# Two of seven block products of a down projection, each split once more into seven half-size products

## The chip, the cores and the metric

The kernel runs on one core of a Trainium2 chip. The metric is the device time of one execution in microseconds; the median of 3 runs before the change was 1494.11 us (1493.38 to 1494.94). The engines are TensorE (PE: matmuls; PEld: loads of the stationary operand), VectorE (DVE), ScalarE (ACT), GpSimd (POOL), and SyncE (SP), whose queue issues the DMA transfers. SBUF is the on-chip memory, PSUM holds the matmul results.

## The reference

One layer of an encoder is applied to two batches, 512 and 1024 rows of 1024 numbers, with the same weights, in 32-bit floats. What matters here is the end of the layer:

```
h = rmsnorm(x, norm_ffn_g)
u = dwconv(h @ w_up, ffn_dw_w, ffn_dw_b)          # 1024 x 5632, convolution over 3 rows
x = x + (silu(u[..., :2816]) * u[..., 2816:]) @ w_down     # 2816 x 1024
return rmsnorm(x, norm_final_g)
```

`w_down` is the down projection: 1536 rows in all, a contraction over 2816 and 1024 columns out.

## The kernel before, in words

**Matmuls.** A product of 32-bit floats is taken as three matmuls in a reduced format. Every operand is split into a high part, which ACT casts, and a low part, which DVE or POOL subtracts; then high x high, high x low and low x high are added up in PSUM. One matmul has a stationary operand of 128 x 128 and a moving operand of up to 512 columns, and loads its own stationary operand.

**Stages.** Attention, convolution and output projection come first, with the prompt's up projection among them. From some 760 us on, the sample's up projection runs as a loop over 22 column tiles `j` (128 gate and 128 value columns; lines 1715 to 1749). It already uses Strassen's method in Winograd's form: `second`, `sixth`, `first`, `seventh`, `fifth`, `fourth`, `third` are seven block products in place of eight. The gated results are written to DRAM by `value_part` (line 1370) in the blocks and block sums that the down projection needs: `ga[i, p]` for product `i` and chunk `p`. For the prompt's rows the same lies in `gt` and `gb`.

**Down projection.** It is again seven block products, in the order 1, 2, 5, 6, 7, 4, 3 (`ORDER`, line 1520). So "the second product" is number 2 and "the sixth" is number 4. Each has 768 rows (512 of the sample's and 256 of the prompt's block), a contraction over 11 chunks of 128 (`NPAIR`), and 512 columns. Its weights are a quarter of `w_down`, or a sum of quarters that DVE makes in place (`operands`, line 1534).

`load_next` (line 1491) takes transfers from a list written out ahead (`ahead`) and issues them on SP's queue; `operands(i, p)` makes the splits for one chunk, in two to three pairs of an ACT cast and a DVE subtraction (lines 1096 and 1092, and 1563 for the prompt's rows); `make(k + lead)` keeps that 4 chunks ahead of TensorE (`LEAD`). `group(i, p, w)` (line 1664) is the six matmuls of one chunk for one of three row blocks `w` (256 rows each), in a two-bank PSUM tile `wide()`, of which there are four. After the last chunk `evacuate` (line 1595) adds the block to the running sums of Winograd's form, on DVE, ACT or POOL. `with_x` adds the residual rows that `load_x1` fetched, one third on DVE and two thirds on POOL. `product(i)` (line 1689) runs the groups, and issues these extra loads and additions at certain chunks of the products 7 and 4.

**Order and buffers.** From the last pass of the loop on, the order of the instructions on TensorE's and SP's queues is that of the program text; in the loop that holds for TensorE only; a planner orders the rest. Buffers come from one list of free slots (`Slots`, line 74: 61 of 2 KB and 15 of 4 KB a partition, and a few others). A tile takes the slot that has been free longest, and its first writer waits until the slot's last reader is done.

Of the kernel before, what the change touches and what calls it, by code (L numbers as in the profile page):

```python
# [9 lines left out]
F32 = mybir.dt.float32  # L10
# [163 lines left out]
def tile_hybrid_encoder(ctx: ExitStack, tc: tile.TileContext, xs, xsT, rel_bias, norm_attn_g, w_in,  # L174
# [1311 lines left out]

    pr, second_half = {}, {}
# [3 lines left out]
    def load_next(n):  # L1491
        for _ in range(n):
            if ahead:
                key, p = ahead.popleft()
                roomy = sum(f[0][0] in "qc" for f in sb.free) > 5
                if (key, p) in second_half:
                    t = second_half.pop((key, p))
                elif key in BRIEF and p % 2 == 0 and p + 1 < NPAIR and roomy:
                    both = sb.tile([2, NT])
                    t, second_half[key, p + 1] = Part(both, 0), Part(both, 1)  # L1500
                    both = None
                else:
                    t = sb.tile([NT])
                pr[key, p] = t
                what, i, n2 = key
                if what == "a":
                    src = ga[i, p][:]
                elif what == "g":
                    n = min(2, NPAIR - 2 * p)
                    for q in range(n):  # L1510
                        j, h = {1: (0, HL), 2: (1, HL), 4: (1, HR)}.get(i, (0, None))
                        src = gb[2 * p + q][:, GB[i], :] if h is None else gt[2 * p + q][:, j, h]
                        nc.sync.dma_start(t[:, q * HT:(q + 1) * HT], src)
# [7 lines left out]
    need = {1: B11, 2: B21, 5: B12, 6: B22, 4: B21, 3: B22}  # L1521
    for i in ORDER:
        for p in range(NPAIR):
            ahead.append((("a", i, 0), p))
            if i in need:
                ahead.append((need[i], p))
            if p % 2 == 0:
                ahead.append((("g", i, 0), p // 2))

# [4 lines left out]
    def operands(i, p):  # L1534
# [4 lines left out]
        a = pr.pop((("a", i, 0), p))  # L1539
        if i == 1:  # L1540
# [17 lines left out]
        hl[i, p] = (split_of(a[:], True), split_of(b[:], True))  # L1558
        if p % 2 == 0:
            g = pr.pop((("g", i, 0), p // 2))  # L1560
            n = slice(0, min(2, NPAIR - p) * HT)
            hi, lo = hp[i, p // 2] = sb.tile([NT], F32R), sb.tile([NT], F32R)
            nc.scalar.copy(hi[:, n], g[:, n])
            sub(lo[:, n], g[:, n], hi[:, n].bitcast(F32))

    steps = [(i, p) for i in ORDER for p in range(NPAIR)]
# [4 lines left out]
    def mm_down(out, i, p, tt):  # L1571
# [7 lines left out]
        nc.tensor.matmul(out, sh[:, c], th[:], start=(p == 0), stop=False)  # L1579
        nc.tensor.matmul(out, sh[:, c], tl[:], start=False, stop=False)  # L1580
        nc.tensor.matmul(out, sl[:, c], th[:], start=False, stop=(p == NPAIR - 1))  # L1581
# [73 lines left out]
    def make(k):  # L1655
        nonlocal made
        while made <= min(k, len(steps) - 1):
            i, p = steps[made]
            operands(i, p)
# [4 lines left out]
    def group(i, p, w, lead=LEAD):  # L1664

        k = ORDER.index(i) * NPAIR + p
# [5 lines left out]
        for q in range(2):  # L1672
            mm_down(pd[w][:, q * NT:(q + 1) * NT], i, p, 2 * w + q)
# [7 lines left out]

    filled = set()
# [5 lines left out]

    def product(i):
        rest = [(p, w) for p in range(2, NPAIR - 2) for w in range(NW3)]  # L1690
# [4 lines left out]
        for p, w in order:  # L1695
# [7 lines left out]
            if i == 4 and p == 2:  # L1703
                load_x1(1, 1)
                fins.append(sb.tile([D]))
                nc.sync.dma_start(fins[0][:], norm_final_g.partition_broadcast(P))
            if i == 4 and p == 4:
                with_x("e", 1, 1)
            if i == 4 and p == 6:
                load_x1(0, 1)  # L1710
            if i == 4 and p == 8:
                with_x("o12", 0, 1)
                load_x1(1, 0)

    for j in range(2, NJ):
# [43 lines left out]
    base = len(steps) - NPAIR  # L1759
# [86 lines left out]
```

## Time and profile before

| | |
|---|---|
| median of 3 runs | 1494.11 us |
| the profiled execution | 1490.76 us |
| its span, first to last instruction | 1489.0 us |
| mean granted TensorE clock | 0.999 |
| TensorE busy | 1471.2 us (99%) |
| DVE / ACT / POOL busy | 1138.2 / 797.0 / 676.7 us |
| matmuls | 6808 |
| moved by DMA | 225.08 MB, mean 151 GB/s |

A row of the profile names the line of the kernel, the engine, the operation, the tiles (out, then in, by their first letters) and the shape, then a count, the busy time and the mean of one in nanoseconds. "Idle before" is the time that the engine waited just before such an instruction, and the arrow names what ended the wait. In a timeline a row begins with its start and its length in microseconds, counted from the start of the span; "x4" are four instructions in one row. A view by stretch gives for each stretch its length and the busy time and the count of instructions of each engine.

### The profile page before, as it was taken

To read this page: it belongs to the slowest core of one execution; us is meant where nothing else is said; L and a number is where in the kernel's file an instruction comes from. 1 tells how busy PE (TensorE), PEld (TensorE's weight loads), DVE (VectorE), ACT (ScalarE), POOL (GpSimd) and SP (SyncE) were. 2 spreads that over 40 slices of the span, in tenths; PEclk is the share of its full clock that TensorE was granted. 3 is DMA by queue.
4 is the path that set the end of the run, shared out by engine and by line. 5 is a ranking of instruction groups with operands and counts; after the bars stand their busy time and mean duration, and the time that the engine had idled before them with its cause. 6 is when DMAs were issued, how large, how long until landed. Compare 5 with 4: busy or idle time off the path is not lost.

```text
span 1489.0 us, 19864 instructions
## 1 busy us (share of the span) xinstructions
PE 1471.2 (99%) x6808; PEld 1219.4 (82%) x6808; DVE 1138.2 (76%) x1616; ACT 797.0 (54%) x1417; POOL 676.7 (45%) x540
## 2 busy tenths in 40 slices
PE   9999999999999999999999999999999999999998
PEld 7788888888888888878888888888887888888886
DVE  5999996788689965766868777777776946569884
ACT  8555656346777776443465554455545633444254
POOL 6953335235665666754336555555544000003345
PEclk9999999999999999999999999999999999999999
DMA  9953246284333346784213333333332672357644
GB/s 315 294 168 86 86 121 194 89 244 130 122 107 121 127 140 209 248 283 168 71 57 107 106 107 106 107 106 102 102 102 84 224 265 85 112 172 232 214 165 170
DMA packets 221761, 225.08 MB, mean 151 GB/s; under 512 B 12331, under 2 KB 161843, under 8 KB 221532
## 3 DMA queue, kind: packets, MB, share of 16 engines
q1 hardware_dynamic: 221660, 223.82, 46.8%
q8 instruction: 53, 0.87, 0.3%
q14 instruction: 48, 0.39, 0.1%
HBM read 164.77 MB, written 60.05 MB: 151 GB/s over the span
## 4 chain that ended last, share of the span: by engine, by line
PE 88%; DVE 3%; DMA 3%; POOL 3%; ACT 2%; issue 1%; SPq 0%; POOLq 0%; ACTq 0%; DVEq 0%
PE w L1229 9%; PE w L1230 9%; PE w L1231 9%; PE w L1580 7%; PE w L1579 7%; PE w L1581 7%; PE u L347 5%; PE u L348 5%; PE u L350 5%; PE b L347 4%; PE b L350 4%; PE b L348 4%; PE u L842 2%; PE u L841 2%; PE u L840 2%; PE a L674 1%
## 5 line engine op out<-in xcount | busy, mean ns | idle before, releaser
L231 POOL TENSOR_TENSOR q<-q,q 128x1024 fp32r<-128x1024 f32 x71 | 172.0, 2428 | 118.9 <-ACT q L230 48.5
L1092 POOL TENSOR_TENSOR q<-q,q 128x512 fp32r<-128x512 f32 x101 | 142.7, 1420 | 148.4 <-ACT q L1215 137.6
L1092 DVE TENSOR_TENSOR h<-h,h 128x512 fp32r<-128x512 f32 (+2 forms) x202 | 157.0, 811 | 66.0 <-ACT h L1096 28.6
L1581 PE MATMUL w<-h,h 128*128 128x512 f32 x462 | 179.7, 389 | 0.0
L1579 PE MATMUL w<-h,h 128*128 128x512 f32 x458 | 178.2, 389 | 0.0
L1580 PE MATMUL w<-h,h 128*128 128x512 f32 x458 | 178.2, 389 | 0.0
L1229 PE MATMUL w<-h,q 128*128 128x512 f32 x448 | 174.9, 390 | 1.6 <-ACT w L1312 1.3
L1231 PE MATMUL w<-h,q 128*128 128x512 f32 x448 | 174.3, 389 | 0.0
L1230 PE MATMUL w<-h,q 128*128 128x512 f32 x426 | 165.8, 389 | 0.0
L402 DVE SCALAR_TENSOR_TENSOR c<-c,cvw,c 128x512 f32<-128x512 f32 x209 | 156.9, 751 | 3.1
L347 PE MATMUL u<-h,q 128*128 128x512 f32 x368 | 146.8, 399 | 1.9 <-DVE h L969 1.9
L348 PE MATMUL u<-h,q 128*128 128x512 f32 x368 | 144.0, 391 | 0.0
L350 PE MATMUL u<-h,q 128*128 128x512 f32 x360 | 141.2, 392 | 0.0
L1089 POOL TENSOR_TENSOR q<-q,q 128x1024 f32<-128x1024 f32 x12 | 32.8, 2742 | 230.0 <-DMA h<-gb 190.0
L1096 ACT CAST h<-h 128x512 fp32r<-128x512 f32 x120 | 71.9, 620 | 99.0 <-DVE h L1092 41.6
L347 PE MATMUL b<-h,q 128*128 128x512 f32 x264 | 104.9, 397 | 0.9 <-DVE q L437 0.9
L348 PE MATMUL b<-h,q 128*128 128x512 f32 x264 | 103.7, 393 | 0.0
L230 ACT CAST q<-q 128x1024 fp32r<-128x1024 f32 (+1 forms) x73 | 75.4, 1038 | 52.6 <-POOL q L231 22.1
L350 PE MATMUL b<-h,q 128*128 128x512 f32 x264 | 103.5, 393 | 0.0
L1581 PEld LDWEIGHTS w<-h,h 128*128 128x128 f32 x462 | 86.7, 188 | 18.0
L1579 PEld LDWEIGHTS w<-h,h 128*128 128x128 f32 x458 | 86.0, 188 | 18.0
L1580 PEld LDWEIGHTS w<-h,h 128*128 128x128 f32 x458 | 86.0, 188 | 17.7
(443 smaller groups left out, 3624.3 us busy)
## 6 DMA issues: line engine op xcount, KB each, us to landing
q<-in_w_up SPq DMA_DIRECT2D x88, 512.0 KB, 4.3
ga<-q SPq DMA_DIRECT2D x64, 256.0 KB, 2.0
h<-ga SPq DMA_DIRECT2D x57, 256.0 KB, 3.5
q<-in_w_in SPq DMA_DIRECT2D x28, 512.0 KB, 5.1
h<-in_w_down SPq DMA_DIRECT2D x52, 256.0 KB, 3.8
q<-in_x_sample SPq DMA_DIRECT2D x15, 512.0 KB, 6.4
h<-qsd SPq DMA_DIRECT2D x23, 256.0 KB, 3.5
x1d<-q SPq DMA_DIRECT2D x11, 512.0 KB, 4.8
```

What stands on the lines that cost most here:

```text
L231: ins = (nc.vector if dve else nc.gpsimd).tensor_tensor(lo[:], raw[:], hi[:].bitcast(F32), op=ALU.subtract)
L347: nc.tensor.matmul(out, whi[:, kc, :], hi[:], start=(kc == 0), stop=False)
L348: nc.tensor.matmul(out, whi[:, kc, :], lo[:], start=False, stop=False)
L350: nc.tensor.matmul(out, wlo[:, kc, :], hi[:], start=False, stop=(kc == KC - 1))
L402: nc.vector.scalar_tensor_tensor(acc[:], src(t), w(t), acc[:], op0=ALU.mult, op1=ALU.add)
L1092: (eng or nc.vector).tensor_tensor(out, a, b, op=ALU.subtract)
L1229: nc.tensor.matmul(out, whi[:, s], hi[:], start=(start and c == 0), stop=False, **go)
L1230: nc.tensor.matmul(out, whi[:, s], lo[:], start=False, stop=False, **go)
L1231: nc.tensor.matmul(out, wlo[:, s], hi[:], start=False, stop=(stop and c == 3), **go)
L1579: nc.tensor.matmul(out, sh[:, c], th[:], start=(p == 0), stop=False)
L1580: nc.tensor.matmul(out, sh[:, c], tl[:], start=False, stop=False)
L1581: nc.tensor.matmul(out, sl[:, c], th[:], start=False, stop=(p == NPAIR - 1))
```

## The change

Products 2 and 4 (`TWO`) are each taken by a second level of the same algorithm. The first ten chunks are paired, so the contraction is split into even and odd chunks, the 768 rows into two halves of 384 and the 512 columns into two of 256. That makes seven inner products in the order 1, 2, 6, 7, 4, 5, 3 (`INNER`), each with 5 chunk pairs (`NQ`), 3 blocks of 128 rows and 256 columns. The eleventh chunk goes through the old `group`.

The sums on the left side for the inner products 5, 6, 7 and 3 are made during the up projection (`two_step`, one call at the end of each pass of the loop, the rest behind it): `two_load` reads the blocks back from DRAM, `two_sums` makes four sums on POOL and stores them in `gl`. The sums of weights for inner product 6 and later are made in `inner` on POOL, four operations of 256 columns for each chunk pair. `inner` also splits the operands, 384 and 256 columns each. `product2` runs the matmuls, with copies and additions in PSUM between the inner products, and keeps the operands 7 sets ahead (`LEAD2`). The extra loads and additions of product 4 now follow its inner products number two to five in that order (`tails`).

```diff
+    TWO = (2, 4)
+    NQ = NPAIR // 2
+    HB = 3 * P
+    gl = {(i, k): dr.tile([P, NQ, HB], F32, name=f"gl{i}_{k}") for i in TWO for k in (5, 6, 7, 3)}
...
+    def two_load(i, q):
+        both = []
+        for p in (2 * q, 2 * q + 1):
+            t = sb.tile([2 * HB])
+            nc.sync.dma_start(t[:, 0:NT], ga[i, p][:])
+            nc.sync.dma_start(t[:, NT:2 * HB], prompt_part(i, p))
+            both.append(t)
+        return both
+
+    def two_sums(i, q, both):
+        (e0, e1), (o0, o1) = ([t[:].rearrange("p (w h c) -> p w h c", h=2, c=P)[:, :, h, :] for h in range(2)] for t in both)
+        gp = nc.gpsimd.tensor_tensor
+        gp(o1, e1, o1, op=ALU.add)
+        gp(e1, e0, e1, op=ALU.subtract)
+        gp(e0, o1, e0, op=ALU.subtract)
+        gp(o0, o0, e0, op=ALU.subtract)
+        for k, src in ((5, o1), (7, e1), (6, e0), (3, o0)):
+            nc.sync.dma_start(gl[i, k][:, q, :].rearrange("p (w c) -> p w c", c=P), src)
...
+    def two_step(j):
+        if two_got:
+            i, q, both = two_got.popleft()
+            two_sums(i, q, both)
+            both = None
+        if two_due and j > 4 * two_due[0][1] + 4:
+            i, q = two_due.popleft()
+            two_got.append((i, q, two_load(i, q)))
...
+                if what == "A":
+                    if (i, n2) in gl:
+                        nc.sync.dma_start(t[:], gl[i, n2][:, p, :])
+                        continue
+                    o, h = {1: (0, 0), 2: (1, 0), 4: (1, 1)}[n2]
+                    src = ga[i, 2 * p + o][:].rearrange("p (w h c) -> p w h c", h=2, c=P)[:, :, h, :]
+                    nc.sync.dma_start(t[:, 0:2 * P].rearrange("p (w c) -> p w c", c=P), src)
+                    nc.sync.dma_start(t[:, 2 * P:HB], prompt_part(i, 2 * p + o)[:, h * P:(h + 1) * P])
+                    continue
...
+    INNER = (1, 2, 6, 7, 4, 5, 3)
...
+    def inner(i, k, q):
+        while (("A", i, k), q) not in pr or (k in (1, 2) and i in need and (need[i], 2 * q + k - 1) not in pr):
+            load_next(1)
+        a = pr.pop((("A", i, k), q))
+        if k in (1, 2):
+            bt[k, q] = weights(i, 2 * q + k - 1)
+        e, o = bt[1, q], bt.get((2, q))
+        if k == 6:
+            t = t1[q] = sb.tile([HT])
+            gp = nc.gpsimd
+            sub(t[:], e[:, QR], e[:, QL], gp)
+            sub(e[:, QR], o[:, QR], e[:, QR], gp)
+            sub(e[:, QL], o[:, QR], t[:], gp)
+            sub(o[:, QL], o[:, QL], e[:, QL], gp)
+            t = None
...
+        ah, al, bb = sb.tile([HB], F32R), sb.tile([HB], F32R), sb.tile([2, HT], F32R)
+        nc.scalar.copy(ah[:], a[:])
+        sub(al[:], a[:], ah[:].bitcast(F32))
+        nc.scalar.copy(bb[:, 0, :], b)
+        sub(bb[:, 1, :], b, bb[:, 0, :].bitcast(F32))
+        h2l[k, q] = ah, al, bb
...
+    tails = {4: {1: last_weights, 2: lambda _=None: with_x("e", 1, 1), 3: lambda _=None: load_x1(0, 1), 4: last_x}}
...
+    LEAD2 = 7
+
+    def product2(i, between):
+        z = {}
+        C11, C12, C21, C22 = (slice(n * HT, (n + 1) * HT) for n in range(4))
+        kept = [sb.tile([2, HT]) for _ in range(NW3)]
+        for n, k in enumerate(INNER):
+            for w in range(NW3):
+                if n == 0:
+                    z[w] = wide()
+                s = {1: C11, 2: C11, 6: C22, 7: C22, 4: C21, 5: C12, 3: C12}[k]
+                out = z[w][:, s]
+                for q in range(NQ):
+                    if len(pr) < CAP and sum(f[0][0] == "h" for f in sb.free) > ROOM:
+                        load_next(1)
+                    make(place[i, k, 0] + (w * NQ + q) // 3 + LEAD2)
+                    ah, al, bb = h2l[k, q]
+                    c = slice(w * P, (w + 1) * P)
+                    go = dict(skip_group_check=True)
+                    nc.tensor.matmul(out, ah[:, c], bb[:, 0, :], start=(k == 1 and q == 0), stop=False, **go)
+                    nc.tensor.matmul(out, ah[:, c], bb[:, 1, :], start=False, stop=False, **go)
+                    nc.tensor.matmul(out, al[:, c], bb[:, 0, :], start=False, stop=(q == NQ - 1), **go)
...
+                if k == 1:
+                    nc.scalar.copy(z[w][:, C22], out)
+                elif k == 6:
+                    nc.scalar.copy(kept[w][:, 0, :], out)
+                elif k == 7:
+                    nc.scalar.copy(z[w][:, C21], out)
+                elif k == 5:
+                    nc.scalar.copy(kept[w][:, 1, :], out)
+                    add(z[w][:, C22], z[w][:, C22], kept[w][:, 1, :])
+                elif k == 3:
+                    add(out, out, kept[w][:, 0, :])
+                out = None
+            if n in between:
+                between[n]()
...
+        for w in range(NW3):
+            group(i, NPAIR - 1, w)
...
     def product(i):
+        if i in TWO:
+            product2(i, tails.get(i, {}))
+            return
...
         third(j)
         split_up(j + 1, 3)
+        two_step(j)
     fill((3, 0), (3, 1), (4, 0), (4, 1))
     sb.free.extend(raws.free)
     value_part(NJ - 1)
+    while two_due or two_got:
+        two_step(NJ)
```

More of the change, by code (lines that the diff above doesn't have):

```diff
@@ L1528, in tile_hybrid_encoder @@
                 ahead.append((("g", i, 0), p // 2))
+    place = {step: n for n, step in enumerate(steps)}
     hl, hp = {}, {}
@@ L1569, in tile_hybrid_encoder, with mm_down @@
     NW3 = 3
-    def mm_down(out, i, p, tt):
+    def mm_down(out, i, p, tt, more=False):
         (sh, sl), (th, tl) = hl[i, p]
@@ L1657, in make @@
         while made <= min(k, len(steps) - 1):
-            i, p = steps[made]
-            operands(i, p)
+            (inner if len(steps[made]) == 3 else operands)(*steps[made])
             made += 1
```

87 lines of the change are left out of this document (58 added, 29 removed).

## Prediction

> **What bounds the kernel now.** I read the page's busy lines and its chain first, then busy time by stretch for the two block products that change, then single instructions there.
>
> ```profile
> span 1489.0 us, 19864 instructions
> PE 1471.2 (99%) x6808; PEld 1219.4 (82%) x6808; DVE 1138.2 (76%) x1616; ACT 797.0 (54%) x1417; POOL 676.7 (45%) x540
> PE 88%; DVE 3%; DMA 3%; POOL 3%; ACT 2%; issue 1%; SPq 0%; POOLq 0%; ACTq 0%; DVEq 0%
> GB/s 315 294 168 86 86 121 194 89 244 130 122 107 121 127 140 209 248 283 168 71 57 107 106 107 106 107 106 102 102 102 84 224 265 85 112 172 232 214 165 170
> ```
> ```profile
> 1212.60:1257.20 44.60, 44.60 (x198) 36.94 (x197) 24.89 (x37) 16.50 (x27) 0.00 (x0) 1.00 0.34 110
> 1391.90:1436.60 44.70, 44.70 (x199) 37.00 (x198) 38.17 (x36) 14.60 (x26) 16.19 (x6) 1.00 0.83 280
> ```
>
> TensorE is busy 99% of the span and carries the chain, at full clock. The second fence is the second and the sixth block product (columns: stretch, length, busy us and count of PE, PEld, DVE, ACT, POOL, then granted clock, DMA share, GB/s). TensorE never stops in either, so fewer TensorE nanoseconds count in full, as long as the operands are ready. They need not stay ready: in the sixth product DVE has 6.5 us left of 44.7.
>
> **TensorE's part.** Starts of full-width matmuls, and of the half-width (256 column) ones that attention has:
>
> ```profile
> 96.30 0.40 PE L674 MATMUL u<-h,h 128*128 128x256 f32 x2
> 96.53 0.64 PE L674 MATMUL a<-h,h 128*128 128x256 f32 x4
> 97.01 0.40 PE L347 MATMUL b<-h,q 128*128 128x512 f32 x1
> ...
> 99.08 0.39 PE L347 MATMUL b<-h,q 128*128 128x512 f32 x1
> ...
> 100.89 0.39 PE L350 MATMUL b<-h,q 128*128 128x512 f32 x1
> ```
> ```profile
> 96.42 0.55 PEld L674 LDWEIGHTS a<-h,h 128*128 128x128 f32 x4
> ```
>
> From 99.08 to 100.89 eight matmuls start: 0.226 us each. Six of half width go from 96.30 to 97.01: 0.118 us each, with a weight load for each. A product before is 11 x 6 x 3 = 198 matmuls, 44.8 us. After, it is 7 products x 3 row blocks x 5 chunk pairs x 3 = 315 of half width, 37.2 us, and 18 full ones for the eleventh chunk, 4.1 us: 41.3 us. The gain is 3.5 us a product, 7 us for both.
>
> The Trainium skill ("TensorE: Matmul & The Clock Gate", Back-to-back issue gap) gives N/2.4 + 2.5 ns, 109 ns and 216 ns here. The trace is 10 ns longer at both widths; by the page an estimate of the gain would be 4.4 us a product instead.
>
> **What the operands cost.** Each of the 35 operand sets of a product (one inner product, one chunk pair) is split: ACT casts 384 and 256 columns, DVE subtracts 384 and 256. Before, 11 steps did that with 512 columns two or three times, 28 pairs.
>
> ```profile
> L1563 ACT CAST h<-h 128x512 fp32r<-128x512 f32 x32 | 19.9, 621 | 27.0 <-DVE h L1092 8.5 <-PE w L1580 6.7 <-DMA h<-gb 5.7
> L1563 ACT CAST h<-h 128x256 fp32r<-128x256 f32 x7 | 2.8, 407 | 14.6 <-DMA h<-gb 6.9 <-DVE h L1092 5.3 <-PE w L1580 2.1
> ```
> ```profile
> 1221.72 1.28 DVE L1092 TENSOR_TENSOR h<-q,h 128x512 fp32r<-128x512 f32 x2
> ```
> ```profile
> 1237.52 0.42 DVE L1092 TENSOR_TENSOR h<-h,h 128x256 fp32r<-128x256 f32 x1 [1.79 <-ACT h L1563]
> ```
> ```profile
> 1389.69 1.23 DVE L1089 TENSOR_TENSOR q<-w,q 128x1024 f32<-128x1024 f32 x1 [0.86 <-PE w L1581]
> 1391.04 4.84 DVE L1092 TENSOR_TENSOR h<-h,h 128x512 fp32r<-128x512 f32 x4
> 1395.80 1.21 DVE L1089 TENSOR_TENSOR q<-w,q 128x1024 f32<-128x1024 f32 x1
> 1396.93 3.48 DVE L1092 TENSOR_TENSOR h<-h,h 128x512 fp32r<-128x512 f32 x2
> ```
> ```profile
> 1388.91 5.21 POOL L1089 TENSOR_TENSOR q<-q,q 128x1024 f32<-128x1024 f32 x2 [16.69 <-DVE q L1089]
> 1397.09 2.77 POOL L1089 TENSOR_TENSOR q<-q,q 128x1024 f32<-128x1024 f32 x1 [2.97 <-DVE q L1089]
> ```
> ```profile
> L1027 POOL TENSOR_TENSOR c<-c,c x7: 730/735/748, 618.6 to 679.5; 128x256 f32<-128x256 f32 x7
> ```
>
> ACT: 0.41 us for 256 columns, between that and 0.62 for 384, say 0.515; 35 x 0.92 = 32 us, twelve copies out of PSUM at about 0.4 (4.8), the eleventh chunk 1.7: 39 us beside 41.3, tight but not first. DVE: two full subtractions take 1.28 us, so one follows the other after 0.60; by the same overlap (0.09) 256 columns take 0.33, 384 between, 0.465: 0.80 us a set, 28.0 us a product. With the eleventh chunk (1.5), six PSUM adds of half width (2.0) and three evacuations of 1.2 (3.6) it is 35 us; DVE alone would fit.
>
> It isn't alone. Four DVE subtractions, 2.4 us of work, took 4.84 beside POOL's additions of 1024 columns, and two took 3.48 instead of 1.28: while POOL works on SBUF operands a DVE subtraction waits, some 2.4 us for each such addition. The new inner product 6 puts four POOL subtractions of 256 columns before each of its five sets (sub-blocks of the weights), 0.735 us each: 20 x 0.735 = 14.7 us, in a stage where POOL did nothing before (second product) or six additions (sixth).
>
> The Trainium skill ("SBUF — State Buffer", SBUF: two separate sides) speaks against the change in the same way: a DVE operation with two SBUF inputs and a GpSimd operation share one port pair, and "the other fully blocks". The trace agrees with 4.84 us for 2.4; by the page the adds that read PSUM (5.6 us a product) would go on beside POOL, which no row above shows, and the sixth product's total below would be 68 us instead of 73.
>
> **When they are due.** Operands are made in program order, seven sets ahead; a set is 9 matmuls, 1.06 us. How far does the machine run ahead of that? The one 256 column cast in the second product is that of chunk 10, which the program makes (four steps ahead) at the group of chunk 6, after 18 groups of 6 x 0.226 us: 1212.6 + 24.4 = 1237.0.
>
> ```profile
> 1237.08 0.41 ACT L1563 CAST h<-h 128x256 fp32r<-128x256 f32 x1 [2.08 <-PE w L1580]
> ```
>
> It started at 1237.08, when TensorE gave a buffer back: the operands are made when the program says, hardly sooner.
>
> Second product, counted from its start: inner product 6 is third, TensorE comes to it at 2 x 5.3 = 10.6 us and wants its last set at 12.0. Its first set (number 10) is made at (10 - 7) x 1.06 = 3.2 us. The last set needs 19 POOL operations, 14.0 us, so 17.2, then a cast and a subtraction: 18.0, 6 us late. The DVE splits of sets 8 to 14 (5.6 us) on the same operands may come between: 11.6 us late. If freed buffers let POOL start 5 us sooner: 1 us late. I take 6: net +2.5 (-2.5 to +8).
>
> Sixth product: sets 0 to 9 also need a DVE subtraction of full width for the weights (0.60), so DVE takes 1.40 a set there. Two of the three 1024 column POOL additions that evacuate the product before lie in it (4.8). Before the last set of inner product 6 is ready, DVE does sets 4 to 9 (8.4) and 10 to 14 (4.0), POOL 4.8 + 14.7: 31.9 us, due at 12.0: 20 us late in strict turns, 14 if half of DVE's part passes beside POOL. Then 20 sets (16.0), adds (2.0) and the two additions of residual rows to finished blocks (each one DVE and two POOL operations of 1024 columns: 2.4 + 9.6 for both) make 30 us against TensorE's 20.8: up to 9 more. The total of the product is DVE 44 + POOL 29 = 73 us, and TensorE needs 41.3. I take a stall of 21 (14 to 29): net +17.5 (+10.5 to +25.5).
>
> Two edits I cost at nothing. The copies and adds in PSUM between inner products: TensorE comes back to a row block after the two others, 2 x 1.77 = 3.5 us, and one such operation takes about 0.4; without that cover (ACT over 3 us behind) each of 18 would show up to 0.4, 7 us. The loads of residual rows move from after chunks 2 and 6 to after the second and the fourth inner product, 12.2 to 10.6 us and 28.5 to 21.2: on SP's queue operand loads stand behind them, some sets ahead; uncovered, 3 MB at 315 GB/s are 10 us.
>
> Transfers: 35 loads of 197 KB replace fifteen of 262 KB, 2.9 MB more. The sixth product moved 280 GB/s x 44.7 us = 12.5 MB; 15.4 MB at the page's highest rate of 315 GB/s are 49 us, under the longer product, but beyond 41.3.
>
> **Up projection.** Its loop gets two loads of 768 columns (four transfers), four POOL operations of 384 columns and four stores in 8 of 20 passes, the last two sets behind it. Priced between 0.735 us (256 columns) and the 1.42 below (512), 1.05: 4.2 us a visit, ahead of the next splits in POOL's queue; the stores wait for POOL in SP's queue, with the weight loads behind them.
>
> ```profile
> L1092 POOL TENSOR_TENSOR q<-q,q 128x512 fp32r<-128x512 f32 x101 | 142.7, 1420 | 148.4 <-ACT q L1215 137.6 <-DVE q L1358 10.8
> ```
> ```profile
> PE w L1229 <- ACT w L1312: 1.3, 1, 1.3
> PE w L1229 <- ACT w L1330: 0.3, 1, 0.3
> ```
>
> POOL idles 148 us before its 101 splits, so there is cover, and TensorE waits 1.6 us in the whole loop (700 to 1165 us), never for POOL. Cover gone, 8 x 4.2 = 34 us. I take 2 (0 to 8).
>
> **Sum.** +2.5 + 17.5 + 2 = +22 us. The profiled execution took 1490.8 us (span 1489.0), 3.3 under the median; 1512.8 on it, 1516 on the median of 1494.1. This case's own range: -2.5 + 10.5 to +8 + 25.5 + 8, 1502 to 1536.
>
> **Rivals.** *The operands keep up.* Everything is ready when TensorE comes, because more free buffers let ACT, DVE and POOL run further ahead, or POOL's short subtractions don't hold DVE up. Then 1494.1 - 7 = 1487. For it: DVE is idle 20 of 44.6 us in the second product. Against: the 73 us of the sixth. It decides at set 14 of the sixth product being ready 12 us after that product starts. 16%.
> *Weight loads bind.* A load shows 0.188 us (86.7 us for 462 in the row below); if half-width matmuls came at that pace, 630 x 0.07 = 44 us more, the splits mostly hidden: 1531. Against: four loads in 0.55 us. 4%.
>
> ```profile
> L1581 PEld LDWEIGHTS w<-h,h 128*128 128x128 f32 x462 | 86.7, 188 | 18.0
> ```
>
> *The loop stalls too*, with the 34 us: 1548. 3%. *Gain and stalls cancel*, the sixth product late by 5 instead of 21: 3%. The forecast case keeps 74%.
>
> **Numbers.** Within 0.2% (3 us, about what a measurement of this kernel tells from no change): the cancelling case and the low edge of mine, 6%; faster 16%; slower 78%. The range 1492 to 1535 leaves out the faster rival and what lies over it.
>
> **What would show it.** TensorE's half-width matmuls 0.118 us apart; DVE, or POOL behind it, as releaser of TensorE at the third inner product; the sixth product some 62 us long, the second about 47; 20 POOL rows of 0.74 to 1.2 us in each. I am wrong if TensorE runs through the sixth product without waiting, or waits for DMA there.

## The result, and the profile after

The changed kernel takes 1554.84 us (median of 4 runs, 1552.76 to 1556.57) beside 1493.95 us before: the ratio is 1.0407, 95% interval 1.0394 to 1.042. It is 61 us slower; the forecast was 22 us slower, with 1535 as its upper end. The profiled execution took 1554.54 us.

The busy lines of the page after, its TensorE and clock digits (40 slices of the span), then busy time by stretch: the up projection's loop of the kernel before, and of the kernel after the loop, the second and the sixth product, each from its first matmul to the first of the next stage. Columns are as in the prediction.

```profile
span 1552.7 us, 21029 instructions
PE 1484.8 (96%) x7078; PEld 1237.1 (80%) x7078; DVE 1202.8 (77%) x1718; ACT 826.2 (53%) x1531; POOL 773.8 (50%) x620
PE   9999999999999999999999999999999979999687
PEclk9999999999999999999999999999999989999899
```
```profile
723.00:1175.90 452.90, 451.13 (x2030) 372.94 (x2029) 346.48 (x359) 232.51 (x350) 212.78 (x152) 1.00 0.33 106
```
```profile
724.60:1195.40 470.80, 456.58 (x2030) 372.86 (x2029) 363.13 (x357) 229.66 (x350) 261.21 (x184) 1.00 0.40 129
1232.15:1297.70 65.55, 48.09 (x334) 44.92 (x333) 50.08 (x89) 39.07 (x93) 18.45 (x20) 0.87 0.54 173
1432.40:1498.80 66.40, 48.94 (x335) 46.91 (x334) 58.20 (x84) 34.05 (x84) 30.93 (x22) 0.87 0.67 227
```

A product before took 198 x 0.226 = 44.8 us. So the loop lost 17.9 us, the second product 20.8 and the sixth 21.6: 60.3 of the 63.7 us by which the span grew. TensorE has holes where it had none: 17.5 us of 65.55 and of 66.40. The mean granted clock, 1.00 before, is 0.87 in both.

What TensorE waited for in the whole run (us in total, times, longest; rows of other stages left out):

```profile
PE w L1813 <- DVE h L1092: 14.5, 6, 4.2
PE w L1229 <- ACT w L1312: 10.4, 7, 2.1
PE w L1812 <- DVE w L1089: 8.0, 3, 4.9
PE w L1812 <- ACT h L1653: 7.8, 3, 4.9
...
PE w L1812 <- ACT w L1819: 2.4, 1, 2.4
PE w L1812 <- ACT q L1699: 2.1, 1, 2.1
```

Lines 1812 to 1814 are the half-width matmuls. They wait for split operands (`h`, L1092 and L1653), but also for additions and copies in PSUM (`w`: L1089, L1819) and for evacuations of the product before (L1699). L1229 is the loop, where L1312 is an ACT copy from one PSUM tile to another.

**Turns of DVE and POOL.** The timeline of the third inner product of the second product, POOL first, then DVE:

```profile
1249.91 1.04 POOL L1092 TENSOR_TENSOR q<-q,h 128x256 f32<-128x256 f32 x1
1250.92 0.91 POOL L1092 TENSOR_TENSOR q<-q 128x256 f32<-128x256 f32 x1
1251.79 1.03 POOL L1092 TENSOR_TENSOR q<-q,h 128x256 f32<-128x256 f32 x1
```
```profile
1249.28 1.08 DVE L1092 TENSOR_TENSOR h<-h,h 128x384 fp32r<-128x384 f32 x1
1250.29 0.95 DVE L1092 TENSOR_TENSOR q<-q,q 128x256 fp32r<-128x256 f32 x1
1251.16 2.08 DVE L1092 TENSOR_TENSOR h<-h,q 128x384 fp32r<-128x384 f32 x2
...
1261.28 0.55 DVE L1092 TENSOR_TENSOR h<-h,q 128x384 fp32r<-128x384 f32 x1
```

Each DVE operation takes about 1 us and each POOL operation about 1 (0.735 in the prediction's row): every one contains a wait for the other engine's. The last row, when POOL had finished, has 0.55 us for the 384 columns that took 1.08. POOL's 20 operations began 9.6 us into the product (1241.74) and were busy for 18.45 us.

**The clock.** Two stretches of 3.4 us in the sixth product, the first right behind a wait of TensorE, the second later:

```profile
1460.20 0.58 PE L1813 MATMUL w<-h,h 128*128 128x256 f32 x1 [2.65 <-DVE h L1092]
```
```profile
1460.20:1463.60 3.40, 3.40 (x16) 3.40 (x17) 1.98 (x1) 0.78 (x2) 3.40 (x2) 0.50 0.76 284
1466.50:1469.90 3.40, 3.40 (x30) 3.40 (x29) 2.30 (x7) 2.96 (x9) 0.00 (x0) 1.00 0.79 237
```

At a granted clock of 0.50, 16 matmuls run where 30 run at 1.00. Busy TensorE time is not full-speed time. Over the half-width matmul starts of the two products, those 0.15 to 0.30 us apart sum to 3.5 us (second) and 5.0 us (sixth) more than 0.12 each would take. With them each product adds up to within 0.3 us: 41.9 us of matmuls at full clock (315 x 0.12 and 18 x 0.226), 19.9 and 19.5 us of waits, and this. The Trainium skill ("TensorE: Matmul & The Clock Gate", Part 1: The HAM clock gate) says that the clock halves after an idle window of about 3.4 us and comes back after as long a busy one; the rows agree in the ratio (0.50) and in the 3.4 us, but not in a wait of 3.4 us as the condition. In this trace a single wait of 2.12 us in the loop (up to 903.93) was followed by 3.4 us at 0.50, and one of 2.10 us (up to 1068.57) by 3.4 us at 1.00. So a shorter wait can set it off, and its length alone doesn't decide.

**The second product's start.** ACT's timeline there, then TensorE's two waits:

```profile
1228.94 0.41 ACT L1653 CAST h<-q 128x256 fp32r<-128x256 f32 x1 [8.64 <-DMA q<-in_w_down]
...
1230.58 1.01 ACT L1699 COPY q<-w 128x1024 f32<-128x1024 f32 x1
1236.27 0.40 ACT L1653 CAST h<-q 128x256 fp32r<-128x256 f32 x1 [4.69 <-DMA q<-in_w_down]
...
1237.00 1.00 ACT L1699 COPY q<-w 128x1024 f32<-128x1024 f32 x1
```
```profile
1238.05 0.38 PE L1812 MATMUL w<-h,h 128*128 128x256 f32 x1 [2.15 <-ACT q L1699]
...
1243.62 0.39 PE L1812 MATMUL w<-h,h 128*128 128x256 f32 x1 [2.36 <-ACT w L1819]
```

A cast waited 4.69 us for weights, the copy that empties a finished PSUM tile stood behind it, and TensorE waited for that tile. SP's queue shows why the weights came late:

```profile
1201.61 0.43 SPq L1565 DMA_DIRECT2D q<-in_w_down  x1
...
1212.04 2.50 SPq L1515 DMA_DIRECT2D gl<-q  x4
...
1220.45 3.75 SPq L1515 DMA_DIRECT2D gl<-q  x4
...
1225.46 0.43 SPq L1565 DMA_DIRECT2D q<-in_w_down  x1
```

For 24 us it issued no load of weights. The loop's last stores stood in it first, then the stores of the last two sets of sums (`gl`), which wait for POOL's sums. The cast that started at 1228.94 had waited 8.64 us for the load issued at 1225.46.

### The profile page after: what moved, and what is told of

Read it like the earlier page. It is cut to its first block, busy times and chain, and to the rows that moved or that the text cites. A ratio compares the mean times of both kernels' runs of the same rounds, so it can differ in the third digit from the quotient of the medians.

```text
span 1552.7 us, 21029 instructions
## 1 busy us (share of the span) xinstructions
PE 1484.8 (96%) x7078; PEld 1237.1 (80%) x7078; DVE 1202.8 (77%) x1718; ACT 826.2 (53%) x1531; POOL 773.8 (50%) x620
## 5 line engine op out<-in xcount | busy, mean ns | idle before, releaser
L1092 DVE TENSOR_TENSOR h<-h,h 128x512 fp32r<-128x512 f32 (+3 forms) x254 | 175.3, 732 | 39.4 <-DMA h<-in_w_down 13.2
L1092 POOL TENSOR_TENSOR q<-q,q 128x512 fp32r<-128x512 f32 x98 | 144.2, 1482 | 109.2 <-ACT q L1215 98.3
L1229 PE MATMUL w<-h,q 128*128 128x512 f32 x452 | 178.4, 395 | 13.1 <-ACT w L1312 10.4
L1676 PE MATMUL w<-h,h 128*128 128x512 f32 x314 | 122.2, 389 | 0.0
L1229 PEld LDWEIGHTS w<-h,q 128*128 128x128 f32 x452 | 85.2, 188 | 35.5 <-ACT w L1312 13.3
L1674 PE MATMUL w<-h,h 128*128 128x512 f32 x286 | 111.3, 389 | 0.0
L1089 POOL TENSOR_TENSOR q<-q,q 128x1024 f32<-128x1024 f32 x9 | 23.6, 2628 | 163.8 <-DVE q L1089 149.4
L1675 PE MATMUL w<-h,h 128*128 128x512 f32 x264 | 102.8, 389 | 0.0
L1231 PEld LDWEIGHTS w<-h,q 128*128 128x128 f32 x436 | 82.3, 189 | 17.4
L1215 ACT CAST q<-q 128x512 fp32r<-128x512 f32 x102 | 62.2, 621 | 61.3 <-DVE h L1092 16.0
L1230 PEld LDWEIGHTS w<-h,q 128*128 128x128 f32 x430 | 81.2, 189 | 16.4
```

The source lines that it names most:

```text
L1092: (eng or nc.vector).tensor_tensor(out, a, b, op=ALU.subtract)
L1229: nc.tensor.matmul(out, whi[:, s], hi[:], start=(start and c == 0), stop=False, **go)
L1230: nc.tensor.matmul(out, whi[:, s], lo[:], start=False, stop=False, **go)
L1231: nc.tensor.matmul(out, wlo[:, s], hi[:], start=False, stop=(stop and c == 3), **go)
```

## The experiments

Each run is one execution, beside one of the kernel before on the same chip (1491.5, 1493.5, 1495.4, 1493.8 and 1492.8 us for the five groups in the order of the labels). The stage ahead of the loop is the same in all, yet the loop began anywhere from 723.0 to 728.1 us. So totals carry some 5 us of that, and what follows is read from the length of a stage, worked out as above: the loop is 452.9 us before and 470.8 in the changed kernel, a product 44.8 before, 65.6 and 66.4 changed. The wait of an inner product is the sum of its gaps of over 0.3 us between matmul starts, each less 0.12.

**The loop.** Four runs. The first keeps `two_step` and takes all seven products as before:

```diff
+    SPLIT = ()
...
-        if i in TWO:
+        if i in SPLIT:
             product2(i, tails.get(i, {}))
```

> The sums of left operands stay in the up projection and behind it, but all seven block products run as before (the stored sums are not used). Theory A (the loop's loss comes from the sums alone, three separate losses add up): 17 to 19 us over before, so about 1512, with TensorE waiting some 15 us for ACT copies in the loop. Rival B (the loop's waits are drawn in by the two changed products, through buffers or transfers that are prefetched): within 3 us of before.

1512.48 us, the loop 471.7 (by stretch, below). The loss lies in the loop's extra work alone.

The second leaves out POOL's four sums:

```diff
-        gp(o1, e1, o1, op=ALU.add)
-        gp(e1, e0, e1, op=ALU.subtract)
-        gp(e0, o1, e0, op=ALU.subtract)
-        gp(o0, o0, e0, op=ALU.subtract)
```

> The whole change, but the four POOL sums of two_sums are left out: the loads and the stores stay, unsummed blocks are stored, so the left operands of four inner products are not the sums. Theory A (POOL's sums hold DVE and ACT up): the loop's 18 us shrink to under 4, total 1537 to 1542. Rival B (two buffers fewer and the extra transfers hold the loop up): the loop keeps over 10 of its 18 us, total over 1547.

1547.39 us, the loop 461.6: the sums are half of the loss, so less than the theory gave them. Its products (67.7 and 67.4) are 1 to 2 us longer than the changed kernel's.

The third is the kernel before with two of the fifteen 4 KB buffers unused from pass `j` = 5, its fourth, to the loop's end:

```diff
+    spare = []
     for j in range(2, NJ):
+        if j == 5:
+            spare += [sb.tile([W2]) for _ in range(2)]
...
+    spare.clear()
```

> The kernel before, with two of the fifteen 4 KB buffers taken out of use from the loop's fourth pass to its end, and nothing else. Theory A (of the loop's 18 us, the 9 us that stayed without the sums come from the two buffers that the loaded blocks hold): 5 to 15 us over before. Rival B (they come from the transfers on SP's queue): within 2 us of before.

1506.05 us, the loop 466.9. Two buffers gone for good cost 14 us, which made held buffers the suspect for the other half. The fourth tests that: the visits take two buffers of 768 columns and hold them for one pass, with no transfer, sum or store, and unsplit products.

```diff
+    SPLIT = ()
...
-            nc.sync.dma_start(t[:, 0:NT], ga[i, p][:])
-            nc.sync.dma_start(t[:, NT:2 * HB], prompt_part(i, p))
             both.append(t)
...
+        return
```

> All products as before, and the loop's eight visits (and the two behind it) only take and hold the two buffers of 768 columns from one pass to the next, without transfers, sums or stores. Nothing is left out of the result. The run with all of the visit's work took 471.5 us in the loop, the one without the sums 461.3, the kernel before 452.7. Theory A: the held buffers make the half that isn't POOL's: the loop takes 458 to 463, 1498 to 1504 in all. Theory B: the transfers in SP's queue do: the loop takes 453 to 455, 1492 to 1497.

1494.29 us, the loop as before. Theory A fell: two buffers kept from one pass to the next cost nothing by themselves. The loop by stretch with buffers only, with transfers as well (sums left out), and with everything, one fence for each kernel:

```profile
726.90:1179.40 452.50, 451.10 (x2030) 372.77 (x2029) 350.25 (x358) 231.98 (x350) 218.47 (x152) 1.00 0.33 107
```
```profile
723.50:1185.10 461.60, 454.84 (x2031) 373.38 (x2030) 355.79 (x358) 231.55 (x351) 218.10 (x152) 1.00 0.42 132
```
```profile
725.90:1197.60 471.70, 457.88 (x2030) 374.05 (x2029) 363.03 (x359) 230.11 (x351) 261.39 (x184) 0.99 0.40 129
```

Loads and stores add 9.1 us, POOL's sums (POOL from 218 to 261 us) another 10.1, or 9.2 by the changed kernel's loop. TensorE's waits for the copy L1312 grow in the same order, 0.8, 5.6 and 10.8 us; what held that copy up was not followed further. Which of the transfers it is, or the order that the planner chose with them, was not tried. And nothing reads the held buffers in the fourth run, whereas in the changed kernel the stores read them: buffers that come free late can still be a part of the 9.1.

**One product at a time.**

```diff
-    TWO = (2, 4)
+    TWO = (2,)
```

> Only the second block product is split, with its sums in 4 visits of the loop in place of 8. Theory A: 9 us in the loop and 16 to 20 in the second product, 1519 to 1523; the first inner product no longer starts late if the transfers behind the loop were what delayed it (then 1516 to 1519). Rival B (the second product loses only beside the sixth's prefetch): under 1508.

1530.11 us, above both ranges: the second product 63.0 (65.6), the loop 469.7. The loop loses 16.8 us with four visits in place of eight, where theory A gave it 9: its loss doesn't go by the number of visits.

With only the sixth split, its sums were made in product 5, the third in order, by one `two_sums` and one `two_load` at every second chunk; that leaves the loop alone:

```diff
-    TWO = (2, 4)
+    TWO = (4,)
...
-    two_due, two_got = deque((i, q) for q in range(NQ) for i in TWO), deque()
+    two_due, two_got = deque(), deque()
...
+            four_step(i, p)
```

> Only the sixth block product is split, and its left sums are made during the third block product, where POOL is idle; in it a transfer is issued only while 4 more buffers are free than before. Theory A: the loop and the second product as before, the sixth keeps its 21 us, 1513 to 1517. Rival B (the sixth is late because of what the earlier parts left behind): under 1503.

1521.68 us, above theory A: the loop is back at 453.0, the sixth product at 68.9, and from the loop to the sixth product it takes 3.2 us more than before, as product 5 now holds the sums. So the loop loses without the split products and the sixth product without the loop's work, each about 20 us; the second product was not tried without the loop's sums.

**The weights' sums on POOL.** First on DVE instead:

```diff
-            gp = nc.gpsimd
+            gp = nc.vector
```

> The whole change, with the four weight sums of each set of inner product 6 on DVE in place of POOL. Theory A (POOL and DVE take turns on SBUF operands, so one set costs four POOL turns of 0.93 us beside two DVE turns): 20 sums at 0.34 us on DVE replace 18.5 us of turns, the third inner product loses 6 to 10 us of its stall in both products, total 1535 to 1545. Rival B (DVE is the full engine, and more work on it costs more): both products longer, total over 1560.

1548.94 us, between the two theories: second product 61.0, sixth 63.4. Taking the sums off POOL is worth 3 to 5 us a product, net of the work that DVE gets for it; DVE alone has no room for the work either (DVE is busy 58 of 63.4 us in the sixth).

Then left on POOL, but made when their second operand is made, five to ten sets ahead:

```diff
-        if k == 6:
...
         h2l[k, q] = ah, al, bb
+        if k == 2:
+            t = t1[q] = sb.tile([HT])
...
```

> The whole change, with the four POOL sums of a chunk pair put five sets sooner into the program, behind the split for inner product 2. Theory A (POOL starts when the program says): the sums begin some 5 us sooner against TensorE, and the stall before inner product 6 falls by 3 to 5 us in each product, total 1546 to 1551. Rival B (the sum of POOL's and DVE's turns is what counts): within 2 us of the changed kernel, or the stall moves ahead to inner product 2.

1541.77 us, below both theories: the second product 61.6, the sixth 59.5. In the second product the waits of the third inner product fall from 11.4 to 1.3 us, but those of the first two rise from 5.0 to 8.1, part of what rival B said. The same applied to the kernel with only the sixth split (its sums stay in product 5, not behind the loop as the expectation has it):

> Only the sixth product in half-size products, its sums made after the loop (1521.7 as it stands), and POOL's four subtractions of weights at the step at which their second operand is made instead of five to ten sets later. Theory A: POOL's chain and DVE's turns beside it set the 16 us stall of the third inner product; with the chain spread over ten sets 7 to 12 us of it go: 1510 to 1515. Theory B: the operations only come in another order in the same total, and DVE's 44 us with POOL's 29 decide: 1518 to 1523.

1514.61 us, sixth product 62.5 in place of 68.9: theory A by the total, but its waits at the third inner product fell only from 16.4 to 12.6 us, not by 7 to 12. When POOL's chain starts is worth 4 to 7 us a product; most of the sixth product's loss stays.

**The second product's start.** The last set of sums for the sixth product holds SP's queue ahead of the first product; its load was moved behind product 1 and its sums behind product 2:

```diff
-    while two_due or two_got:
-        two_step(NJ)
+    later = [two_due.pop()]
+    two_step(NJ)
...
+        if i == 1:
+            later.append(two_load(*later[0]))
+        if i == 2:
+            two_sums(*later[0], later.pop())
```

> The whole change, with the last set of sums for the sixth product loaded only after the first block product and summed and stored after the second, in place of both right behind the loop. Theory A (its stores wait for POOL on SP's queue some 10 us, with the operand loads of the second product behind them): the first inner product of the second product starts in time, its 5 us stall falls under 2, total 1548 to 1551. Rival B (SP's own pace, three transfers of 0.4 to 0.6 us for a set of 1.06 us, makes the loads late): the stall stays over 3, total within 3 us of the changed kernel.

1560.02 us, the second product 68.2, and 5.8 us of waits in its first two inner products (5.0 in the changed kernel): theory A's gain did not come. But SP then requests the next weights at 1219.45, 15.3 us ahead of the product in place of 6.7, and no cast there waits for weights any more. ACT waits for another late load, the left operand of the third inner product, with the copies L1699 behind it:

```profile
1236.10 0.51 ACT L1651 CAST q<-h 128x384 fp32r<-128x384 f32 x1 [10.16 <-DMA h<-gl]
```

The run with only the second product split, which has one set of sums fewer there too, shows the same: no wait for weights, 8.68 us for `gl`. So the last sums do hold up the weights; with that gone, the next load takes their place. Next, one transfer for each half-size operand in place of two:

```diff
-                    nc.sync.dma_start(t[:, 0:2 * P].rearrange("p (w c) -> p w c", c=P), src)
-                    nc.sync.dma_start(t[:, 2 * P:HB], prompt_part(i, 2 * p + o)[:, h * P:(h + 1) * P])
+                    nc.sync.dma_start(t[:], ga[i, 2 * p + o][:, 0:HB])
```

> The changed kernel, but the operand of the inner products 1, 2 and 4 (row blocks x 384) comes as one contiguous transfer of 384 columns instead of two, one of them in pieces of 512 bytes: two issues of 0.53 and 0.60 us on SP's queue become one. It leaves out the right choice of columns, so these inner products multiply other numbers. Theory A: the issues on SP (1.56 us a set against 1.06 us of TensorE) make the operands late; then the first inner product of the second block product, which stands still 5 us, starts without that, and the whole is 4 to 8 us below the changed kernel's 1554.8: 1547 to 1551. Theory B: the casts wait for the tiles of the down weights, which are requested late for another reason (SP's queue held until the loop's end); then 1553 to 1556.

1559.11 us, the second product 65.1. The waits moved from the first inner product (2.3 us to 0.3) to the second (2.7 to 4.2), so the pace of SP's issues alone is not the cause. (The sixth took 72.4, 6 more than changed; unexplained.) Next, with the weights' sums sooner, eight loads of 192 KB less:

```diff
+                        if n2 in same:
+                            idle[key, p], pr[key, p] = t, same[n2]
+                            continue
+                        same[n2] = t
...
```

> The run with both products split and the weights' subtractions sooner (1541.8), but inner products 1 and 2 of the second product load one operand of 384 columns each and use it for all five sets: eight loads of 192 KB less in the first ten sets, buffers held as before. It leaves out the right rows for eight sets. Theory A: ten sets of 448 KB in 10.6 us are 430 GB/s, and the core moved about 240 GB/s there, so the bytes make the first sets late: the 8.1 us of stall in the first two inner products fall to 4 or less, 1533 to 1537. Theory B: the wait is latency behind a buffer that TensorE gives back late; the stall stays at 6 or more, 1539 to 1543.

1537.12 us, the second product 54.3 (61.6 without this edit), yet the waits of its first two inner products are 7.4 us as against 8.1. Theory A's gain came, but at the later inner products (6.5 us of waits before, 2.8 now) and not at the place that it named; for the start theory B stands. Last, the copies out of PSUM on DVE:

```diff
-            nc.scalar.copy(fresh("u")[:], z[:])
+            nc.vector.tensor_copy(fresh("u")[:], z[:])
...
-                    nc.scalar.copy(z[w][:, C22], out)
+                    nc.vector.tensor_copy(z[w][:, C22], out)
```

> The run with both products split and the weights' subtractions sooner (1541.8), but DVE, not ACT, copies the first product's blocks out of PSUM (three operations of 1024 columns) and C22 after the first inner products. Theory A: ACT's order sets the second product's start (these copies stand behind casts that wait for weights), so 4 us or more of the 8.1 us of wait in its first two inner products go: 1533 to 1538. Theory B: the operands are late whatever the copies do, and the wait goes from the copy to the operand: 6 us or more of it stay, 1540 to 1544.

1545.82 us, outside both ranges, but the second product takes 61.8 us as against 61.6, and the waits at its start grew from 8.1 to 12.0 us: by the stage it is theory B's side. TensorE's wait there is now one of 11.6 us, still for a copy:

```profile
1251.08 0.55 PE L1812 MATMUL w<-h,h 128*128 128x256 f32 x1 [11.63 <-DVE w L1819]
```

On either engine the copy stands behind splits that wait for weights. What would bring all loads of the start in time was not tried.

**PSUM between inner products.** The second level's sums there, six copies and six additions of a product, left out:

```diff
-                elif k == 6:
-                    nc.scalar.copy(kept[w][:, 0, :], out)
...
-                elif k == 5:
-                    nc.scalar.copy(kept[w][:, 1, :], out)
-                    add(z[w][:, C22], z[w][:, C22], kept[w][:, 1, :])
-                elif k == 3:
-                    add(out, out, kept[w][:, 0, :])
```

> The changed kernel without the sums of the second level in PSUM: the copies after inner products 6, 5 and 3 (nine a product would be six copies and six additions for three row blocks) are left out, the two copies that start C22 and C21 stay. The output lacks these sums. Theory A: these operations stand in ACT's and DVE's queues behind splits of sets that are made ahead, and TensorE waits for them at the last two inner products (3.5 us and about 5 us), which the prediction costed at nothing: 6 to 10 us below the changed kernel's 1554.8, 1545 to 1549. Theory B: those waits are for operands that are late anyhow, and move to them: 1552 to 1556.

1551.51 us, half a us below theory B's range. By stage the second product gets 3.9 us shorter (61.6) and the sixth 2.3 longer (68.7). In the sixth the wait for the additions is gone, 5.3 us ahead of the last inner product, but 2.9 us of waits for splits stand in its place, and those at the third inner product grew from 8.5 to 12.4 us.

**Residual rows in the sixth product.** On the kernel with only the sixth split and the sums sooner, TensorE waits 4.22 us for the addition in PSUM that follows the sixth inner product, at the start of the last one (the 271st of 315 half-width matmuls; the expectations place this wait at the sixth). POOL's, DVE's and TensorE's timeline there:

```profile
1439.24 5.33 POOL L1089 TENSOR_TENSOR q<-q,c 128x1024 f32<-128x1024 f32 x2 [12.13 <-DMA c<-x1d]
```
```profile
1439.68 5.18 DVE L1092 TENSOR_TENSOR h<-q,h 128x256 fp32r<-128x256 f32 x2
1444.78 4.03 DVE L1092 TENSOR_TENSOR h<-h,h 128x384 fp32r<-128x384 f32 x9
1448.74 0.42 DVE L1089 TENSOR_TENSOR w<-w,h 128x256 f32<-128x256 f32 x1
```
```profile
1449.21 0.58 PE L1812 MATMUL w<-h,h 128*128 128x256 f32 x1 [4.22 <-DVE w L1089]
```

Two splits (0.75 us) took 5.18 beside POOL's additions; the PSUM addition behind them came 4.2 us late. First the second addition was written later, behind the last inner product:

```diff
-    tails = {4: {1: last_weights, 2: lambda _=None: with_x("e", 1, 1), 3: lambda _=None: load_x1(0, 1), 4: last_x}}
+    tails = {4: {1: last_weights, 2: lambda _=None: with_x("e", 1, 1), 3: lambda _=None: load_x1(0, 1), 6: last_x}}
```

> As the run with only the sixth product split and the weights' subtractions sooner, and the second addition of residual rows (one DVE and two POOL operations of 1024 columns) stands after the last inner product instead of after the fifth of seven. Theory A: it is these POOL operations that hold DVE's splits, and behind them the additions in PSUM, for the 5 us stall at the sixth inner product: 3 to 5 us below that kernel. Theory B: the stall is that of the PSUM additions standing behind splits, whatever POOL does: within 1.5 us of that kernel.

1522.27 us, and it decides nothing: the planner left the addition at its place in POOL's and DVE's order, and only the load written behind it came later. Then the first addition was left out:

```diff
-    tails = {4: {1: last_weights, 2: lambda _=None: with_x("e", 1, 1), 3: lambda _=None: load_x1(0, 1), 4: last_x}}
+    tails = {4: {1: last_weights, 2: lambda _=None: xd.pop((1, 1)), 3: lambda _=None: load_x1(0, 1), 4: last_x}}
```

> The run with only the sixth product split and the weights' subtractions sooner (1514.6), and the first addition of residual rows to a finished block (one DVE and two POOL operations of 1024 columns) is left out, its loads are kept; that block lacks these rows in the output. Theory A: POOL's two operations hold DVE's splits, and the PSUM additions behind those, so the 4.4 us stall at the sixth inner product goes: 1508 to 1511. Theory B: the PSUM additions are late by their place behind the splits of seven sets alone; the stall stays at 3 us or more, 1512 to 1516.

1517.52 us, the wait stays (4.29 us): it is not the first addition. Then the second:

```diff
-        with_x("o12", 0, 1)
+        xd.pop((0, 1))
```

> The run with only the sixth product split and the weights' subtractions sooner (1514.6, its sixth inner product waits 4.4 us), and the second addition of residual rows (one DVE and two POOL operations of 1024 columns) is left out, its loads are kept; that block lacks these rows in the output. Theory A: POOL's two operations (5.3 us) hold two of DVE's subtractions for 5.2 us, and ACT's copies and DVE's additions in PSUM behind them, so the 4.4 us go: 1508 to 1511. Theory B: the PSUM additions are late by their place behind the splits alone; 3 us or more of the wait stay, 1512 to 1517.

```profile
1443.10 0.75 DVE L1092 TENSOR_TENSOR h<-q,h 128x256 fp32r<-128x256 f32 x2
1443.77 4.03 DVE L1092 TENSOR_TENSOR h<-h,h 128x384 fp32r<-128x384 f32 x9
1447.72 0.42 DVE L1089 TENSOR_TENSOR w<-w,h 128x256 f32<-128x256 f32 x1
```
```profile
1397.70:1460.20 62.50, 45.86 (x335) 44.22 (x334) 53.30 (x82) 32.10 (x79) 30.22 (x21) 0.89 0.68 224
```
```profile
1400.80:1458.60 57.80, 45.36 (x334) 43.96 (x333) 46.49 (x78) 31.32 (x78) 24.02 (x19) 0.88 0.66 224
```

The same two splits take 0.75 us, TensorE doesn't wait there, and the product falls from 62.5 to 57.8 us (the last two fences: with the addition, without). By the stage it is theory A. The total, 1514.95, lies in theory B's range and doesn't show the gain: from the loop to the sixth product the run took 2.7 us more than the one with the addition, and behind the sixth product 1.8 us more, longer there than any other run with only the sixth split. Why is open, so a part of the 4.7 us may only have moved.

No run came below the kernel before, and none pointed to one that would: without any wait the gain is 3.5 us a product.

## Why the prediction was wrong, point by point

The direction and the engine were right: DVE behind POOL heads TensorE's waits. The size was not: +61 for +22. In the three stages it is +60.3, 38.3 more than forecast: 15.9 from the loop, 18.3 from the second product and 4.1 from the sixth.

- **TensorE's gain, 3.5 us a product.** Right: half-width matmuls start 0.12 us apart at full clock. That answers the rival "Weight loads bind" too.
- **"Up projection ... I take 2 (0 to 8)": the step that failed first, +17.9 measured.** It argued that POOL idles 148 us before its splits. A total says nothing of the passes in which the work falls: POOL's sums cost 9 to 10 us, and one of them took 1.23 us where it priced 1.05. The stores and loads in SP's queue, which it named but gave no term, cost 9.1. Its 34 us of "cover gone" are POOL's sums alone, so that the total lies halfway to them is chance. The rival "The loop stalls too" (1548) came nearest in the end, with half of its stall in the loop and a late second product that it didn't have.
- **"Second product ... I take 6: net +2.5": failed, +20.8 measured.** It took the operands to be made in time up to the third inner product. The casts waited for weights, which SP's queue requested late behind the last sums; TensorE waited 5.0 us in the first two inner products, and POOL's chain began at 9.6 us, not 3.2. The chain's 20 operations took 18.45 us, not 14.7, as each waits for DVE's. The third inner product's waits were 11.4 us on top of the 5.0, so even the upper end that the prediction worked out (11.6 us late) was too low. The rest are 3.5 us of waits for additions in PSUM and 3.5 us lost at half clock, both answered below.
- **"Two edits I cost at nothing": failed for the PSUM operations.** It gave 3.5 us of cover, with ACT over 3 us behind as the condition for losing it; ACT and DVE were. It put the loss at 0.4 us for each operation; the rows show single waits up to 4.9 us, 8.0 in all for additions in PSUM and 2.4 for a copy. Leaving the sums out gave 3.9 us in the second product and cost 2.3 in the sixth, where other waits took their place, so how much of the 10.4 is theirs alone stays open.
- **Sixth product, +17.5 (+10.5 to +25.5): right in the total, +21.6 measured, in part by luck.** The working "DVE 44 + POOL 29 = 73 us" beside 41.3 foresaw the engines. But of the 14 to 20 us at the third inner product 8.5 came, with 5.7 at the second; 5.3 are the wait for additions in PSUM, costed at nothing, and 5.0 the half clock, not foreseen. The row additions were in that sum; the product was 4.7 us shorter where the second of them was taken out.
- **"which no row above shows": a reading that missed its own rows.** DVE's addition out of PSUM at 1389.69 took 1.23 us inside POOL's additions of 1388.91 (5.21 us), as against 1.21 at 1395.80 with POOL still. Such additions do go on beside POOL; without their 5.6 us the 73 would be 67, not 68.
- **Not in the prediction: the clock.** A wait can cost more than its length: 8.5 us of the two products are time lost to matmuls at half clock behind waits.
- **ACT, 39 us: right**, 39.07 in the second product.

Transfers as the bound of the sixth product were weighed at 49 us; it took 66 at 227 GB/s, and TensorE waited there for DVE (12.5 us) and an ACT cast (4.9), never directly for a transfer.

## What to carry to other kernels

Where one engine is the bound at 99%, a change that saves 7 us of its work can be paid for many times by work on the others: ask for each stage what those engines can still take, and not for the whole. An engine's idle total is no cover; look for the pass and the place in its order. A short copy or addition in PSUM between matmuls can cost the lateness of everything that stands ahead of it in its queue, and so can a waiting store ahead of a load; the matmul engine may then restart at half speed.

## What the hardware showed that was not expected

- Granted clock 0.50 for 3.4 us behind waits of TensorE (16 matmuls where 30 fit), once behind a single wait of 2.12 us. Before the change TensorE doesn't wait in the two products, so they couldn't show it.
- Two engines that both read SBUF operands hold each other on every operation: DVE's 384 columns took 1.08 us beside POOL and 0.55 when POOL was still, and 0.75 us of DVE work took 5.18 beside two POOL operations of 1024 columns. The Trainium skill ("SBUF — State Buffer", SBUF: two separate sides) says of the shared port pair that the loser of a turn "fully blocks"; the 5.18 beside 5.33 us agrees. An addition that reads PSUM does go on: in the kernel with only the sixth split and the sums sooner, one started at 1399.93 and took its 1.21 us inside a POOL addition (1399.69 to 1402.27). But the PSUM addition at 1448.74 above was late all the same, since it stands behind the blocked splits in DVE's order.
- Of the program rather than the chip: two 4 KB buffers of fifteen, unused for most of the loop, cost 14 us; two kept from one pass to the next, with nothing that reads them, cost nothing.
